# Three quarters of the second MLP's down-projection as 2x2 blocks in seven products

## The chip, the core and the metric

One core of one Trainium2 chip runs the whole program; the seven other cores are idle. The metric is the device time of one execution in microseconds (us). Five engines work side by side, each through its own list of instructions in a fixed order: TensorE (PE in the profile), VectorE (DVE), ScalarE (ACT), GpSimd (POOL) and SyncE (SP). SP issues the loads from DRAM, POOL issues other transfers besides small computations.

## The reference

A trunk of two layers on one sequence of 512 tokens of width 1024, in float32. Layer 0 mixes tokens by an mLSTM, layer 1 by a gated short convolution; each is followed by an MLP with squared ReLU. RMS norms stand before and behind each part.

```python
def sqrelu_mlp(x, w_up, w_down):
    h = jax.nn.relu(x @ w_up)
    return (h * h) @ w_down
...
        h = sqrelu_mlp(rms_norm(x, g[2]), w_mlp_up[i], w_mlp_down[i])
        x = x + rms_norm(h, g[3])
```

`w_up` is 1024 x 4096 and `w_down` 4096 x 1024. The change concerns `(h * h) @ w_down` of layer 1, where `h * h` is 512 x 4096.

## The kernel before

**Numbers.** Every large product is made from two reduced-precision halves: `split` (L79) writes the upper half of a tile on ScalarE (a cast, L80) and the remainder on VectorE (L81). `mm3` (L112) then makes three matmuls: upper times upper, upper times lower, lower times upper (L115, L116, L117). So each factor costs a ScalarE and a VectorE instruction, and each product three matmuls.

**Buffers.** `u` (15 tiles of 8 KB per partition) holds split weights, split activations and accumulators; `hb` (4 of 8 KB) the split hidden activations; `raw` (7 of 4 KB) weights as loaded; `t2` (8 of 2 KB) intermediate values. PSUM has eight banks of 512 columns: four named `pu`, two `pd`, two `pt`. A tile of a pool that is full waits until its oldest user is through.

**Up-projection.** The 4096 hidden columns are made by eight quads of 512 columns each (class `Quad`, L848). A quad is already a 2x2 block product in seven multiplications: the activations stand as seven factors (class `Seven`, L199: `a11`, `a12`, `a22`, `p1`, `n2`, `r3`, `p4`; seven `u` tiles that stay for the whole MLP), the weights as four blocks of 512 x 256 with four sums that VectorE forms from raw tiles (L957, L963, L981, L992). `prod` (L835) is one such product: 24 matmuls of 256 columns. Three quads begin early, during the layer before (`begin`, L885, the early product). For each finished quarter `take` (L1023) applies ReLU on ScalarE (L1026) where the values come from PSUM, squares on VectorE (L1029), and splits into an `hb` tile.

**Down-projection.** `down(g)` (L1040) multiplies the 512 hidden columns of quad g with 512 rows of `w_dn`: two column halves, four token tiles, four k tiles, three matmuls each, 96 matmuls of 512 columns (out `pd`). The weights come as four pieces of 128x1024, loaded (L98) and split. The result is written to accumulators `ys` by ScalarE for g = 0 (L1063) and added by VectorE after that (L1065). The order is quad 0, quad 1, `down(0)`, quad 2, `down(1)`, ..., `down(5)`, quad 7; `last_product` (L280) then takes the last 1024 hidden columns together with the norm and the store.

**Sums in DRAM.** During the first MLP, POOL's queue forms some sums of the convolution's weights in DRAM, for its quads (class `Sums`, L350): a tiny transfer (`mark`) that waits for an accumulator, so that the rest starts at the intended time, then copies from DRAM to DRAM and transfers that add. One such piece is made behind the first half of each of six `down(g)`.

**What sets the order.** The text above is traced in program order; a scheduler then fixes each engine's list when the program is built, from priorities and its own idea of durations. Each engine works its list strictly in order. A few items are put off by a count of TensorE time (`step`, `put_off`).

Of the kernel before, what the change touches and what calls it, by code (L numbers as in the profile page):

```python
# [39 lines left out]
def tile_hybrid_trunk(  # L40
# [309 lines left out]
    class Sums:  # L350

        def __init__(self, name, wm, c0, c1, shape, key, quads):
            self.all = dram.tile([2, 512] + shape, F32, name=name)

            def src(kh, c):
                m = wm[kh * 512 : (kh + 1) * 512, c : c + D]
                if len(shape) > 1:
                    m = m.rearrange("k (b s) -> k b s", s=512)[:, :, 0:256]  # L360
                return m

            self.blocks = src(0, c0), src(0, c1), src(1, c0), src(1, c1)
            for i, c in enumerate(quads):
                made[key, c] = [
                    self.of(n, i).rearrange("(p q) m -> q p m", q=P) for n in range(2)
                ]

        def of(self, n, i):
            f = self.all[n]  # L370
            return f[:, i, :] if len(f.shape) > 2 else f[:, i * 256 : (i + 1) * 256]

        def make(self, r0, r1, mark):

            a, b, c, d = (blk[r0:r1] for blk in self.blocks)
            f = [self.all[n, r0:r1] for n in range(2)]
            first = self.all[:, r0]
            first = first[:, 0, 0:1] if len(first.shape) > 2 else first[:, 0:1]
            nc.gpsimd.dma_start(first, mark)
            for dst, blk in zip(f, (a, b, d, c)):  # L380
                nc.gpsimd.dma_start(dst, blk)
            for dst, blk in list(zip(f, (b, d))) + []:
                nc.gpsimd.dma_start(dst, blk, accum_op=ALU.add, max_dma_last_dim=D)

    made = {}
# [404 lines left out]
        put_pair(hT, j, pr)  # L790

    wc = w_in_conv[0]
    cx = Sums("cx", wc, D, 2 * D, [D], "conv", [D + p * 256 for p in range(4)])
    og = Sums("og", wc, 0, 256, [2, 256], "conv", [0, 512])
    later = [(cx, p * P, (p + 1) * P) for p in range(4)] + [(og, 0, 256), (og, 256, 512)]

    def scores_and_core(t):
        scores(t)
# [218 lines left out]
    def mlp(i, xT, gain_of, tail_of, ends=False, ahead=None):  # L1017

        NG = FF // P // G
        hs = [None] * (FF // P // 2)  # L1020

        def quad(g):
            def take(nh, half, c, o):  # L1023
                j = 2 * g + nh
                if o is not None:
                    nc.scalar.activation(c, o, AF.Relu)  # L1026
                else:
                    o = c
                nc.vector.scalar_tensor_tensor(  # L1029
                    out=c, in0=o, scalar=0.0, in1=c, op0=ALU.max, op1=ALU.mult  # L1030
                )
# [8 lines left out]
        def down(g):  # L1040
            if g == 0:
                ys.extend(token_tiles())
            for hf, cs in enumerate(halves()):
# [6 lines left out]
                for t in range(NT):  # L1050
# [12 lines left out]
                        nc.scalar.copy(yh, o)  # L1063
                    else:
                        nc.vector.tensor_tensor(out=yh, in0=yh, in1=o, op=ALU.add)  # L1065
# [6 lines left out]
        gy, tail = gain_of(), tail_of()  # L1072
        quads[0].run_first()
        quads[1].run(True)
        for g in range(NG - 2):
            down(g)
            quads[g + 2].run(g + 2 < AHEAD)
            if g == NG - 4:
                fetch_x()
        last_product(w_dn[i], FF - D, hs[-(KO // 2) :], gy, tail, ys, ends, ahead)  # L1080


# [109 lines left out]
```

## Time and profile before

| | us |
|---|---|
| median of 3 runs | 1098.38 (1097.92 to 1098.44) |
| the profiled execution, its own time | 1098.65 |
| its span, first to last instruction | 1096.9 |
| TensorE busy | 1076.6 (98%) |
| VectorE busy | 744.8 (68%) |
| ScalarE busy | 503.9 (46%) |
| second MLP: early products from, quads 0 and 1 until, last product from | 748.9, 797.0, 1045.1 |

A group's row names the line, the engine, the operation, out<-in with shapes and count, then busy time and mean duration in ns, then the idle time of the engine ahead of these instructions and what ended it. A row of the order of time begins with start and duration, both in us, and ends with the wait in brackets. A row by window gives, for each engine, busy time and the instructions that touch the window, then granted TensorE clock, the busy share of the 16 DMA engines, and GB/s. Matmuls overlap, so the start-to-start distance counts, not their duration.

### The profile page before, as it was taken

Reading aid. Unit: us, or ns where it says so; the run is one execution under the profiler, and the core shown is the slowest. Engines: PE = TensorE matmul, PEld = TensorE weight load, DVE = VectorE, ACT = ScalarE, POOL = GpSimd, SP = SyncE. Lnnn points to the kernel's source line nnn. Section 1 sums busy time; section 2 is a strip of 40 time slices with the busy share of each in tenths; the row PEclk is TensorE's granted clock in tenths of the full one; section 3 lists DMA queues with packets and bytes.
Section 4 is the critical chain, followed back from the end, with each engine's and each line's share of the span. In section 5 each row is a group of like instructions: output and inputs, shape, how many; then the busy total and the mean of one; then the engine's idle time right before and its main releaser. Section 6 shows DMA issues by size and latency. Waiting matters only on the chain.

```text
span 1096.9 us, 16084 instructions
## 1 busy us (share of the span) xinstructions
PE 1076.6 (98%) x6531; PEld 948.9 (87%) x6531; DVE 744.8 (68%) x996; ACT 503.9 (46%) x780; POOL 98.1 (9%) x144
## 2 busy tenths in 40 slices
PE   8999999999999999999999999999999999999997
PEld 5878887789899898898888999988988988989986
DVE  5561567489775775766769978859967567565843
ACT  6431445355543353343556655646554424423521
POOL 1100010110001001011042000011000000000011
PEclk9999999999999999999999999999999999999999
DMA  8420273226386366385624554713533413415201
GB/s 269 135 77 1 63 244 126 86 97 192 116 230 178 110 173 156 109 256 134 211 76 138 188 194 137 249 58 124 175 125 97 154 51 104 136 56 193 96 20 58
DMA packets 114624, 147.90 MB, mean 135 GB/s; under 512 B 5845, under 2 KB 84469, under 8 KB 114550
## 3 DMA queue, kind: packets, MB, share of 16 engines
q1 hardware_dynamic: 101830, 118.03, 34.0%
q0 software_dynamic: 12720, 28.84, 9.4%
q8 instruction: 51, 0.84, 0.3%
q14 instruction: 23, 0.19, 0.1%
HBM read 138.47 MB, written 20.97 MB: 145 GB/s over the span
## 4 chain that ended last, share of the span: by engine, by line
PE 42%; DVE 4%; issue 2%; ACT 1%; DMA 1%; POOL 0%; POOLq 0%; DVEq 0%; ACTq 0%
PE pd L115 8%; PE pd L116 8%; PE pd L117 8%; PE pu L116 6%; PE pu L115 6%; PE pu L117 6%; DVE u L81 1%; DVE u L274 1%; PE pt L261 0%; ACT u L80 0%; DMA raw<-in_w_in_conv_dram 0%; POOL small L173 0%; DVE t L1029 0%; DMA xd<-u 0%; DVE hb L81 0%
## 5 line engine op out<-in xcount | busy, mean ns | idle before, releaser
L81 DVE TENSOR_TENSOR u<-raw,u 128x1024 fp32r<-128x1024 f32 (+1 forms) x270 | 320.7, 1200 | 126.5 <-ACT u L80 126.1
L80 ACT CAST u<-raw 128x1024 fp32r<-128x1024 f32 (+1 forms) x270 | 273.6, 1029 | 205.3 <-PE pd L117 159.8
L115 PE MATMUL pu<-u 128*128 128x256 f32 (+1 forms) x1112 | 336.8, 303 | 0.7 <-ACT u L80 0.7
L116 PE MATMUL pu<-u 128*128 128x256 f32 (+1 forms) x1112 | 335.5, 302 | 0.4 <-DVE u L81 0.4
L117 PE MATMUL pu<-u 128*128 128x256 f32 (+1 forms) x1112 | 334.4, 301 | 0.0
L115 PE MATMUL pd<-u,hb 128*128 128x512 f32 (+1 forms) x648 | 255.0, 393 | 1.5 <-DVE t L1029 0.9
L116 PE MATMUL pd<-u,hb 128*128 128x512 f32 (+1 forms) x648 | 254.1, 392 | 0.0
L117 PE MATMUL pd<-u,hb 128*128 128x512 f32 (+1 forms) x648 | 254.1, 392 | 0.0
L115 PEld LDWEIGHTS pu<-u 128*128 128x128 f32 x1112 | 210.2, 189 | 10.1 <-ACT u L80 1.1
L116 PEld LDWEIGHTS pu<-u 128*128 128x128 f32 x1112 | 209.9, 189 | 9.9 <-DVE u L81 1.3
L117 PEld LDWEIGHTS pu<-u 128*128 128x128 f32 x1112 | 210.0, 189 | 8.7 <-DVE u L81 0.3
L115 PEld LDWEIGHTS pd<-u,hb 128*128 128x128 f32 x648 | 121.8, 188 | 31.0 <-DVE t L1029 1.7
L117 PEld LDWEIGHTS pd<-u,hb 128*128 128x128 f32 x648 | 121.8, 188 | 28.0
L116 PEld LDWEIGHTS pd<-u,hb 128*128 128x128 f32 x648 | 121.8, 188 | 27.5 <-DVE u L81 0.6
L115 PE MATMUL pd<-u 128*128 128x256 f32 x312 | 88.3, 283 | 3.3 <-ACT pu L888 2.9
L116 PE MATMUL pd<-u 128*128 128x256 f32 x312 | 87.4, 280 | 0.0
L117 PE MATMUL pd<-u 128*128 128x256 f32 x312 | 87.2, 281 | 0.0
L1065 DVE TENSOR_TENSOR u<-u,pd 128x512 f32<-128x512 f32 x80 | 54.6, 683 | 36.6 <-PE pd L117 36.5
L181 ACT ACTIVATE junk<-u 128x512 bf16<-128x512 f32 (+1 forms) x49 | 30.5, 623 | 79.5 <-DVE u L318 58.1
L80 ACT CAST hb<-t 128x512 fp32r<-128x512 f32 x80 | 49.0, 620 | 32.5 <-DVE t L1029 26.6
L115 PEld LDWEIGHTS pd<-u 128*128 128x128 f32 x312 | 58.8, 188 | 4.4 <-ACT pu L888 3.6
L116 PEld LDWEIGHTS pd<-u 128*128 128x128 f32 x312 | 58.8, 189 | 0.0
(179 smaller groups left out, 864.9 us busy)
## 6 DMA issues: line engine op xcount, KB each, us to landing
raw<-in_w_mlp_up_dram SPq DMA_DIRECT2D x76, 512.0 KB, 5.0
raw<-in_w_mlp_down_dram SPq DMA_DIRECT2D x64, 512.0 KB, 4.0
raw<-in_w_in_mlstm_dram SPq DMA_DIRECT2D x24, 512.0 KB, 4.7
raw<-in_w_in_conv_dram SPq DMA_DIRECT2D x21, 512.0 KB, 4.9
cx<-in_w_in_conv_dram POOLq DMA_DIRECT2D x16, 512.0 KB, 6.5
xd<-u POOLq DMA_DIRECT2D x12, 512.0 KB, 3.1
u<-xd POOLq DMA_DIRECT2D x12, 512.0 KB, 6.9
raw<-in_w_out_mlstm_dram SPq DMA_DIRECT2D x8, 512.0 KB, 4.2
```

The lines of the kernel that those rows point to most:

```text
L80: hi = nc.scalar.copy(dst_hi, src)
L81: lo = nc.vector.tensor_tensor(out=dst_lo, in0=src, in1=dst_hi.bitcast(F32), op=ALU.subtract)
L115: nc.tensor.matmul(o, lh, rh, start=first, stop=False, skip_group_check=True)
L116: nc.tensor.matmul(o, lh, rl, start=False, stop=False, skip_group_check=True)
L117: nc.tensor.matmul(o, ll, rh, start=False, stop=last, skip_group_check=True)
L181: nc.scalar.activation(junk(n), src, AF.Square, scale=float(D) ** -0.5, accum_out=ms[:, i : i + 1])
L274: nc.vector.scalar_tensor_tensor(out=xt[:, hs], in0=y, scalar=r, in1=xt[:, hs], op0=ALU.mult, op1=ALU.add)
L1065: nc.vector.tensor_tensor(out=yh, in0=yh, in1=o, op=ALU.add)
```

## The change

For layer 1's MLP the first six `down(g)` become three calls of `down7(c)`, each for 1024 hidden columns (quads 2c and 2c+1) and 1024 rows of `w_dn`, ahead of quads 2, 4 and 6; quads 6 and 7 and `last_product` stay as they were. In `down7` the hidden activations are 2x2 blocks: `a11`, `a12`, `a21`, `a22`, with token halves as rows and quads as columns, and the weights 2x2 blocks of 512 x 512. Seven products of blocks replace eight: product 1 is a11 with the upper left weight block (banks x, two `pd`), 2 is a12 with the lower left one (added in x), 3 to 7 use differences of hidden blocks and sums of weight blocks (banks z, two `pt`; y, two `pu`; o, two `pd`). A product takes two loads and two splits of weights (two k tiles each), one split of a hidden block, and 2 token tiles x 4 k tiles x 3 = 24 matmuls of 512 columns. `minus` is a negated copy from banks to banks by ScalarE (L1151 of the new text), `add` adds banks to the accumulators (VectorE, L1143; for block 0, where a quarter is written for the first time, ScalarE, L1141), `plus` adds raw weights (VectorE, L1118), and L1160, L1164, L1173, L1178 are the differences of hidden blocks, formed in place.

For this the squares of quads 0 to 5 are written, unsplit, to two `u` tiles (`hb7`) by ScalarE (`take7`: ReLU, then Square), and VectorE's squaring and splitting there fall away. Two (blocks 1, 2) or four (block 0) sums of weight blocks are formed in DRAM on POOL's queue, behind the second half of the first MLP's six `down(g)`.

```diff
-            for dst, blk in list(zip(f, (b, d))) + []:
+            adds = list(zip(f, (b, d)))
+            if self.n > 2:
+                adds += [(f[2], f[0]), (f[3], f[2])]
+            for dst, blk in adds:
                 nc.gpsimd.dma_start(dst, blk, accum_op=ALU.add, max_dma_last_dim=D)
...
+    dn = [
+        Sums(f"dn{c}", n, [dn_block(c, kh, nh) for kh in range(2) for nh in range(2)], [512])
+        for c, n in enumerate((4, 2, 2))
+    ]
...
+        1: [(d, *r) for d in dn for r in halves_of],
...
+            def take7(nh, half, c, o):
+                h = hb7[g % 2][:, half, 2 * nh : 2 * nh + 2, :]
+                nc.scalar.activation(c, c if o is None else o, AF.Relu)
+                nc.scalar.activation(h, c, AF.Square)
+
+            if i == 1 and g < 6:
+                take = take7
...
-                if i == 0 and hf == 0 and later:
-                    sm, r0, r1 = later.pop(0)
-                    sm.make(r0, r1, yh[0:2, 0:1])
+                if i == 0 and later[hf]:
+                    sm, r0, r1 = later[hf].pop(0)
+                    sm.make(r0, r1, yh[0:4, 0:1])
+
+        def down7(c):
...
+            def mult(os, raws, fh, first):
+                for hh, raw in enumerate(raws):
+                    w = unit([2, 2, 512], F32R)
+                    split(w[:, 0], w[:, 1], raw)
+                    for u in range(2):
+                        step(PROD / 4)
+                        for k in range(2):
+                            mm3(
+                                os[u],
+                                [fh[:, s, 2 * hh + k, u * P : (u + 1) * P] for s in range(2)],
+                                [w[:, s, k, :] for s in range(2)],
+                                first and hh == 0 and k == 0,
+                                hh == 1 and k == 1,
+                            )
...
+            (a11, a12), (a21, a22) = a
+            x = two(pd)
+            mult(x, loads(dn_block(c, 0, 0)), factor_h(a11), True)
+            y = two(pu)
+            minus(y, x)
+            mult(x, loads(dn_block(c, 1, 0)), factor_h(a12), False)
+            add(0, 0, x)
+            tt(out=a21, in0=a21, in1=a22, op=ALU.subtract)
+            z = two(pt)
+            f5 = summed(0)
+            mult(z, f5, factor_h(a21), True)
+            tt(out=a11, in0=a11, in1=a21, op=ALU.subtract)
+            add(1, 1, z)
+            if sums.n > 2:
+                f6 = summed(2)
+            else:
+                d = loads(dn_block(c, 1, 1))
+                plus(f5, d)
+                f6 = f5
+            mult(y, f6, factor_h(a11), False)
+            tt(out=a12, in0=a12, in1=a11, op=ALU.subtract)
+            add(1, 0, y)
+            if sums.n > 2:
+                d = loads(dn_block(c, 1, 1))
+            mult(z, d, factor_h(a12), False)
+            tt(out=a11, in0=a22, in1=a11, op=ALU.subtract)
+            add(1, 0, z)
+            mult(y, summed(1), factor_h(a11), False)
+            o = two(pd)
+            minus(o, y)
+            add(1, 1, y)
+            if sums.n > 2:
+                f4 = summed(3)
+            else:
+                plus(f5, loads(dn_block(c, 1, 0)))
+                f4 = f5
+            mult(o, f4, factor_h(a22), False)
+            add(0, 1, o)
...
+            for k in range(2):
+                hb7[k] = unit([2, 4, 256])
+                nc.gpsimd.memset(hb7[k][:, 0, 0, 0:1], 0.0)
         quads[0].run_first()
         quads[1].run(True)
...
+            for g in range(2, NG):
+                if g % 2 == 0:
+                    down7(g // 2 - 1)
+                quads[g].run(g < AHEAD)
+            fetch_x()
```

**How the lists move.** Up to the second MLP, PE, DVE, ACT and SP keep the same rows in the same order; they keep them again in the last product. Three places follow; names ending in a number are buffers.

VectorE in the second `down(g)` and the quad after it, before: additions of `pd` banks to the accumulators (L1065) stand between the sums and splits of the next quad's weights.

```order
L81 TENSOR_TENSOR hb_7699<-t2_7730,hb_7699 128x512
L1065 TENSOR_TENSOR u_7429<-u_7429,pd_7745 128x512
L81 TENSOR_TENSOR u_7902<-raw_7867,u_7902 128x1024
L1065 TENSOR_TENSOR u_7429<-u_7429,pd_7759 128x512
L963 TENSOR_TENSOR raw_7867<-raw_7867,raw_7930 128x1024
L981 TENSOR_TENSOR raw_7869<-raw_7869,raw_7930 128x1024
L1065 TENSOR_TENSOR u_7430<-u_7430,pd_7773 128x512
L81 TENSOR_TENSOR u_7933<-raw_7867,u_7933 128x1024
```

VectorE now, at products 6 and 7 of block 1 (z is pt_8223 and pt_8224, y is pu_8179 and pu_8180; hb_8347 and hb_8392 are the hidden blocks of products 6 and 7, u_8395 and u_8410 the weights of product 7):

```order
L1143 TENSOR_TENSOR u_7461<-u_7461,pt_8223 128x512
L81 TENSOR_TENSOR hb_8347<-u_7138,hb_8347 128x1024
L1143 TENSOR_TENSOR u_7461<-u_7461,pt_8224 128x512
L1118 TENSOR_TENSOR raw_8225<-raw_8225,raw_8386 128x1024
L1118 TENSOR_TENSOR raw_8227<-raw_8227,raw_8388 128x1024
L81 TENSOR_TENSOR hb_8392<-u_7140,hb_8392 128x1024
L81 TENSOR_TENSOR u_8395<-raw_8225,u_8395 128x1024
L1143 TENSOR_TENSOR u_7462<-u_7462,pu_8179 128x512
```

The addition of a finished bank stands ahead of the split that the next product needs, and two sums of weights ahead of the next.

VectorE now, from there into quad 4 (o is pd_8380 and pd_8381; u_8431, u_8462 and u_8493 are the weights of quad 4's first three products):

```order
L81 TENSOR_TENSOR u_8410<-raw_8227,u_8410 128x1024
L1143 TENSOR_TENSOR u_7462<-u_7462,pu_8180 128x512
L81 TENSOR_TENSOR u_8431<-raw_8427,u_8431 128x1024
L970 TENSOR_TENSOR raw_8427<-raw_8427,raw_8429 128x1024
L1143 TENSOR_TENSOR u_7462<-u_7462,pd_8380 128x512
L1143 TENSOR_TENSOR u_7462<-u_7462,pd_8381 128x512
L81 TENSOR_TENSOR u_8462<-raw_8427,u_8462 128x1024
L994 TENSOR_TENSOR raw_8429<-raw_8429,raw_8490 128x1024
L976 TENSOR_TENSOR raw_8427<-raw_8427,raw_8490 128x1024
L81 TENSOR_TENSOR u_8493<-raw_8427,u_8493 128x1024
```

The additions of product 7's banks stand ahead of the splits for the quad's second and third products.

POOL in the first MLP, before, behind the first two `down(g)`: one piece of the convolution's sums `cx` each.

```order
L379 DMA cx<-u 2x1
L381 DMA cx<-in_w_in_conv_dram 128x1024 x2
L383 DMA cx<-in_w_in_conv_dram 128x4x256 x2
L379 DMA cx<-u 2x1
L381 DMA cx<-in_w_in_conv_dram 128x1024 x2
```

POOL now, at the same place (dn_711 is the tensor of block 0's sums):

```order
L364 DMA cx<-u 2x1
L366 DMA cx<-in_w_in_conv_dram 128x1024 x2
L371 DMA cx<-in_w_in_conv_dram 128x4x256 x2
L364 DMA dn_711<-u 4x1
L366 DMA dn_711<-in_w_mlp_down_dram 256x512 x4
L371 DMA dn_711<-in_w_mlp_down_dram 256x2x256 x2
L371 DMA dn_711<-dn_711 512x256 x2
L364 DMA cx<-u 2x1
```

Behind each of the convolution's pieces stands one of the sums for `w_dn`: eight transfers in the first two rounds, four in the four later ones.

More of the change, by code (lines that the diff above doesn't have):

```diff
@@ L350, in tile_hybrid_trunk, with __init__, make @@
     class Sums:
[L354 to L373, printed above, removed]
+        def __init__(self, name, n, blocks, shape):
+            self.n, self.blocks = n, blocks
+            self.all = dram.tile([n, 512] + shape, F32, name=name)
+        def make(self, r0, r1, marks):
             a, b, c, d = (blk[r0:r1] for blk in self.blocks)
[L376 removed]
+            f = [self.all[n, r0:r1] for n in range(self.n)]
             first = self.all[:, r0]
             first = first[:, 0, 0:1] if len(first.shape) > 2 else first[:, 0:1]
[L379 removed]
+            nc.gpsimd.dma_start(first, marks[0 : self.n, :])
             for dst, blk in zip(f, (a, b, d, c)):
                 nc.gpsimd.dma_start(dst, blk)
[L382 removed]
+            adds = list(zip(f, (b, d)))
+            if self.n > 2:
+                adds += [(f[2], f[0]), (f[3], f[2])]
+            for dst, blk in adds:
                 nc.gpsimd.dma_start(dst, blk, accum_op=ALU.add, max_dma_last_dim=D)
@@ L1065, in down, with factor_h, load_rows, loads @@
                         nc.vector.tensor_tensor(out=yh, in0=yh, in1=o, op=ALU.add)
-                if i == 0 and hf == 0 and later:
-                    sm, r0, r1 = later.pop(0)
-                    sm.make(r0, r1, yh[0:2, 0:1])
+                if i == 0 and later[hf]:
+                    sm, r0, r1 = later[hf].pop(0)
+                    sm.make(r0, r1, yh[0:4, 0:1])
+        def down7(c):
+            tt = nc.vector.tensor_tensor
+            a = [[hb7[k][:, half] for k in range(2)] for half in range(2)]
+            sums = dn[c]
+            def factor_h(src):
+                f = big.tile([P, 2, 4, 256], F32R, tag="hb", name="hb", bufs=NHB)
+                split(f[:, 0], f[:, 1], src)
+                return f
+            def load_rows(src, hh):
+                raw = raw_tile([2, 512])
+                nc.sync.dma_start(
+                    raw, src[hh * 256 : (hh + 1) * 256, :].rearrange("(k p) m -> p k m", p=P)
+                )
+                return raw
+            def loads(src):
+                return [load_rows(src, hh) for hh in range(2)]
+            def summed(n):
+                return loads(sums.all[n])
+            def plus(rs, qs):
+                for r, q in zip(rs, qs):
+                    tt(out=r, in0=r, in1=q, op=ALU.add)
+            def mult(os, raws, fh, first):
[11 more added lines that the diff above has]
+                                hh == 1 and k == 1,
+                            )
+            written = set()
+            def add(nh, half, os):
+                for u in range(2):
+                    yh = ys[2 * half + u][:, nh * 512 : (nh + 1) * 512]
+                    if c == 0 and (nh, half) not in written:
+                        nc.scalar.copy(yh, os[u])
+                    else:
+                        tt(out=yh, in0=yh, in1=os[u], op=ALU.add)
+                written.add((nh, half))
+            def two(bank):
+                return [bank() for _ in range(2)]
+            def minus(os, qs):
+                for o, q in zip(os, qs):
+                    nc.scalar.mul(o, q, -1.0)
+            (a11, a12), (a21, a22) = a
[31 more added lines that the diff above has]
+                f4 = summed(3)
+            else:
+                plus(f5, loads(dn_block(c, 1, 0)))
+                f4 = f5
+            mult(o, f4, factor_h(a22), False)
+            add(0, 1, o)
```

40 lines of the change are left out of this document (32 added, 8 removed).

## The prediction

> **What bounds the kernel now.** I read the page's first two parts, then the busy time by stage, then the groups of the second MLP by shape, then the order of time on each engine.
>
> ```profile
> span 1096.9 us, 16084 instructions
> PE 1076.6 (98%) x6531; PEld 948.9 (87%) x6531; DVE 744.8 (68%) x996; ACT 503.9 (46%) x780; POOL 98.1 (9%) x144
> PE   8999999999999999999999999999999999999997
> DVE  5561567489775775766769978859967567565843
> ```
>
> TensorE (PE) is busy from end to end; VectorE (DVE) is next at 68%, with its fullest slices where the second MLP starts. Busy is not peak, so I measured the pitch. The second MLP's second down-projection runs from 834.19 to 856.57 and the quad after it to 876.55:
>
> ```profile
> core 0: us, PE busy (x) PEld busy (x) DVE busy (x) ACT busy (x) POOL busy (x), PEclk, DMA share, GB/s
> 834.19:856.57 22.38, 22.38 (x98) 18.04 (x97) 15.70 (x20) 5.94 (x7) 0.00 (x0) 1.00 0.11 37
> 856.57:876.55 19.98, 19.98 (x170) 19.98 (x169) 13.86 (x16) 10.92 (x14) 0.00 (x0) 1.00 0.56 175
> 740.00:800.00 60.00, 58.60 (x446) 55.72 (x444) 56.31 (x75) 34.67 (x58) 4.26 (x6) 1.00 0.46 150
> ```
>
> A down-projection is 96 matmuls of 512 columns (two of the 98 only reach in), a quad 168 of 256: 22.38 / 96 = 0.2331 us and 19.98 / 168 = 0.119 us each, without a gap, at clock 1.00. So this stage is bound by the number of matmuls. VectorE needs 13.9 of a quad's 20 us there, but 56.3 of 60 us while the MLP starts, and even that costs TensorE 1.4 us only.
>
> **The matmuls removed.** Six down-projections are 576 matmuls. Three blocks of seven products, each 2 token tiles x 4 k tiles x 3, are 504, of the same 512 columns. 72 x 0.2331 = 16.8 us less TensorE time. By the Trainium skill (TensorE: Matmul & The Clock Gate, "Wait — 56ns, not 53.3ns?") matmuls start N / 2.4 GHz + 2.5 ns apart, 0.2158 us here; by it the saving would be 15.5 us, and the trace does not agree. I go by the trace.
>
> **What is added on VectorE and ScalarE (ACT).**
>
> ```profile
> L81 DVE TENSOR_TENSOR u<-raw,u 128x1024 fp32r<-128x1024 f32 x85 | 103.0, 1221 | 53.2 <-ACT u L80 53.1
> L1065 DVE TENSOR_TENSOR u<-u,pd 128x512 f32<-128x512 f32 x40 | 27.3, 683 | 18.4 <-PE pd L117 18.4
> L81 DVE TENSOR_TENSOR hb<-t,hb 128x512 fp32r<-128x512 f32 x32 | 21.8, 683 | 0.2 <-ACT hb L80 0.2
> L1029 DVE SCALAR_TENSOR_TENSOR t<-t 128x512 f32<-128x512 f32 x20 | 13.7, 685 | 0.2
> L963 DVE TENSOR_TENSOR raw<-raw 128x1024 f32<-128x1024 f32 x7 | 8.5, 1219 | 0.0
> L80 ACT CAST u<-raw 128x1024 fp32r<-128x1024 f32 x84 | 86.7, 1048 | 86.3 <-PE pd L117 76.4 <-DVE raw L957 7.3 <-DVE raw L992 1.1
> L1026 ACT ACTIVATE t<-pu 128x512 f32<-128x512 f32 x10 | 6.0, 598 | 14.5 <-PE pu L117 14.5
> L888 ACT ACTIVATE pu<-pu 128x512 f32<-128x512 f32 x6 | 3.5, 582 | 8.8 <-PE pu L117 8.8
> ```
> ```profile
> 807.84 3.50 DVE L81 TENSOR_TENSOR u<-raw,u 128x1024 fp32r<-128x1024 f32 x3 [5.98 <-ACT u L80]
> 736.92 1.29 DVE L81 TENSOR_TENSOR u<-pt,u 128x512 fp32r<-128x512 f32 x2 [1.00 <-ACT u L80]
> 758.02 0.58 ACT L888 ACTIVATE pu<-pd 128x512 f32<-128x512 f32 x1
> 758.54 2.93 ACT L80 CAST u<-raw 128x1024 fp32r<-128x1024 f32 x3
> 834.19 0.40 PE L115 MATMUL pd<-u,hb 128*128 128x512 f32 x1
> 834.42 0.40 PE L116 MATMUL pd<-u,hb 128*128 128x512 f32 x1
> ```
>
> Instructions in a row overlap a little: three splits take 3.50 us, not 3.67, so one more of 1024 elements costs (3.50 - 1.22) / 2 = 1.14 us and one of 512 costs 1.29 - 0.68 = 0.61; on ScalarE (2.93 - 1.05) / 2 = 0.95 for 1024, and for 512 the 0.52 from 758.02 to 758.54. A matmul lasts 0.40 us at a pitch of 0.23, so its result is there 0.17 us after the next could start.
>
> VectorE in blocks 1 and 2: 14 weight splits, 7 splits of hidden blocks, 4 differences of hidden blocks, 4 sums of weights, 29 x 1.14 = 33.1, and 12 additions into the accumulators, 12 x 0.61 = 7.3: 40.4 us beside 168 x 0.2331 = 39.2 us of TensorE. Block 0 has its weight sums from DRAM, and ScalarE writes eight of its twelve additions: 25 x 1.14 + 4 x 0.61 = 30.9 us. In exchange quads 0 to 5 lose four squarings and four splits each: 11 x 1.14 + 2 x 0.61 = 13.8 us instead of 18.6, in 20.0. A block with its two quads holds VectorE 58.5, 68.0 and (quads 6 and 7 keep their squarings) 77.6 us, against 79.2 us of TensorE; before, 8 x 1.14 + 16 x 0.61 + 2 x 18.6 = 56.1 against 84.7. ScalarE, with the squares (priced as L1026) and four negated copies (L888), has 21 x 0.95 + 4 x 0.52 = 22 us in a block (26 in block 0) and 7 x 0.95 + 12 x 0.52 = 13 in a quad, so it has room.
>
> The sum fits; the order decides. Of the 15 u buffers the seven activation factors take 7, the hidden blocks 2 and the accumulators 2; four are left, two products' worth, where six were left before. I walked VectorE's rows through block 1 with the durations above, each no earlier than the cast, the product or the freed buffer it needs, from TensorE's first product at 0:
> - First three products: the casts reach VectorE at 1.7, 3.95 and 7.35 us; the parts for products 3 and 4 are split by 8.5 and 15.8, needed from 11.2 and 16.8.
> - Product 5 (needed from 22.4): its hidden block is split at 20.4.
> - Product 6 (28.0): VectorE must first add bank z, complete at 26.8, and then split the hidden block: 28.6. TensorE's order puts the four matmuls that need only the upper half first, until 28.9: covered by 0.3.
> - Product 7 (33.6): two weight sums, the hidden split and the weight split end at 33.7; the first matmul needs only the cast: covered by 0.1.
> - The quad after it: the additions of product 7's banks end at 40.0; then come a split, two sums, a cast and a split, 45.5, where TensorE wants the lower half at 45.3 or so: 0.3 us lost.
>
> Blocks 0 to 2 thus lose 0, 0.3 and 0.3 us by the walk. For handovers that no row prices I take 0.7 us for each of blocks 1 and 2, 1.4 together. The bounds are a gain of 0.5 (VectorE's easier start of the MLP) and 5 us a block (first rival). The negated copy ahead of product 2 is ready at 4.9 and 6.4 us, the banks are wanted at 5.6 and 7.0: nothing, and 1.2 us per bank without this cover.
>
> ```profile
> 751.73 0.28 PE L117 MATMUL pd<-u 128*128 128x256 f32 x1
> 753.23 0.39 PE L115 MATMUL pd<-u 128*128 128x256 f32 x1 [1.22 <-ACT pu L888]
> 759.03 0.56 POOL L173 TENSOR_TENSOR small<-small,mhalf 128x1 f32<-128x1 f32 x1 [1.73 <-DVE small L168]
> ```
>
> POOL's two one-column memsets that claim the hidden blocks wait for the first early product, over at 752; the reciprocal root for the fourth token tile, which stands behind them, starts at 759: nothing.
>
> **What is added in the first MLP.** Only POOL's queue changes there: 32 transfers of 512 KB from DRAM to DRAM and six marks, behind the ones for the convolution.
>
> ```profile
> 296.00:338.00 42.00, 42.00 (x241) 36.60 (x241) 31.57 (x35) 18.97 (x25) 5.84 (x8) 1.00 0.66 185
> 338.00:380.00 42.00, 42.00 (x265) 37.68 (x264) 28.91 (x33) 16.85 (x21) 4.18 (x5) 1.00 0.54 148
> q0 software_dynamic: 8497, 13.62, 29.5%
> raw<-in_w_mlp_down_dram SPq DMA_DIRECT2D x23, 512.0 KB, 4.2
> raw<-in_w_mlp_up_dram SPq DMA_DIRECT2D x16, 512.0 KB, 8.6
> cx<-in_w_in_conv_dram POOLq DMA_DIRECT2D x12, 512.0 KB, 6.5
> og<-in_w_in_conv_dram POOLq DMA_DIRECT2D x8, 512.0 KB, 6.7
> u<-xd POOLq DMA_DIRECT2D x4, 512.0 KB, 7.3
> 333.39 0.56 POOL L379 DMA_DIRECT2D cx<-u  x1 [25.34 <-DVE u L1065]
> 341.44 2.65 POOL L383 DMA_DIRECT2D cx<-in_w_in_conv_dram  x2 [5.13 <-DMA cx<-in_w_in_conv_dram]
> 343.71 7.92 SPq L865 DMA_DIRECT2D raw<-in_w_mlp_up_dram  x4
> 354.14 23.72 SPq L98 DMA_DIRECT2D raw<-in_w_mlp_down_dram  x4
> 362.94 1.22 DVE L957 TENSOR_TENSOR raw<-raw 128x1024 f32<-128x1024 f32 x1
> ```
>
> The rows of queues and issues are of the 210 us from 310 to 520: q0 took 62 us of all engines for 12 + 8 + 4 transfers of 512 KB, 2.6 us each. The first two rounds of 42 us get eight more, 20.7 us, beside 0.66 x 42 = 27.7 and 22.7: 48 and 43 of 42, full. The four later rounds get 10.3 on about 23. So in two rounds weights land late. Their cover: loads issued from 343.71 on are first read at 362.94, 19 us later, for a landing of 8.6; those from 354.14 wait for buffers, not for engines. Twice the landing still fits: I take 0.5 us, bounds 0 and 4 a round. By the Trainium skill (DMA: Bandwidth & Descriptors, "Queues, rings and completion order") each engine goes round the queues packet by packet, so that q1 would keep half, and 8.6 would become at most about 17 us, an estimate from that rule; the up weights, which land in 8.6 us beside the convolution's sums where the down weights take 4.2, agree with it, and no run here shows a full round.
>
> **The sum.** Against the profiled run's own 1098.65 us (span 1096.9, 1.75 outside): 1098.65 - 16.8 + 1.4 + 0.5 = 1083.75. That run is 0.27 above the median of the three; forecast **1083.5 us**.
>
> **The rivals.**
> - VectorE sets the pace. If in blocks 1 and 2 nothing overlaps, 29 x 1.22 + 12 x 0.683 = 43.6 us, 4.4 more than TensorE; quads 6 and 7 then need 20.3, 0.3 more each. 1083.5 - 1.4 + 9.4 = 1091.5. For it: 77.6 of 79.2 us, and fewer buffers. Against it: 56.3 of 60 us cost 1.4 us.
> - Slower than before: the banks' handover. Four products of a block (2, 5, 6, 7) write banks that ScalarE or VectorE must read first. At 753.23 TensorE does wait for such a copy (L888), 1.22 us. The other bank's six matmuls cover 1.4 us. If the reader stands two splits behind, a handover costs 0.17 + 2 x 1.14 + 0.68 - 1.4 = 1.7 us, and some 0.3 at the second bank: 12 x 2.0 = 24, so 1083.5 - 1.4 + 24 = 1106. It decides from 16.8 / 12 = 1.4 us a handover on. Against it: the walk has readers at most 0.4 us late.
> - The sums in DRAM starve the first MLP: 8 us in its two full rounds, 1083.5 - 0.5 + 8 = 1091. Against it: the lead of 19 us.
>
> **How the numbers follow.** Forecast 0.68, VectorE 0.15, starved loads 0.07, handover 0.07; 0.03 for a mixture that just cancels the gain. Faster by over 0.2% (about what this kernel's runs can tell from no change): 0.68 + 0.15 + 0.07 = 0.90; within it 0.03; slower 0.07. The range starts at the full saving, 1098.38 - 16.8 - 0.5 = 1081, and takes in the first and third rival: 1081 to 1092; the forecast's own is 1081 to 1087.
>
> **What would show it.** Right: 72 matmuls fewer; each block near 39.3 us (block 0) and 39.5 to 40 (1 and 2); VectorE over 95% busy in blocks 1 and 2; TensorE's few waits there on L81 of hidden blocks and at the third product after a block; DMA share near 1 from 300 to 380 with TensorE still full. Wrong: blocks of 43 us or more with idle time before VectorE's splits (first rival), waits of over 1 us on L1151 or L1143 (second), or TensorE idle between 300 and 380 (third).

## The result, and the profile after

| | before | after |
|---|---|---|
| median of the runs, us | 1098.41 (1097.92 to 1098.65, 4 runs) | 1086.72 (1083.68 to 1087.24, 4 runs) |
| profiled execution, us (its span) | 1098.65 (1096.9) | 1083.68 (1082.0) |
| matmuls | 6531 | 6459 |

The ratio is 0.9888, with a 95% interval of 0.987 to 0.9907: 11.7 us faster, and 1086.72 us against 1083.5 forecast. The profiled run gained 15.0 us, the three others (1086.61, 1086.83, 1087.24) about 12. The same kernel in a later series had a median of 1088.26 (1087.47 to 1089.06; ratio 0.991, 0.9897 to 0.9924). So 3 to 5 us come and go, and the questions are where, and why.

The page of the change, its head and the DMA row of the slices:

```profile
span 1082.0 us, 16129 instructions
PE 1060.0 (98%) x6459; PEld 934.8 (86%) x6459; DVE 775.5 (72%) x995; ACT 555.8 (51%) x847; POOL 133.6 (12%) x186
...
DMA  9420274225399998798953556632555424524601
```

TensorE is full as before, on 72 matmuls fewer. The slices from the twelfth to the twentieth (297 to 541 us), where the first MLP runs, show DMA at 0.7 or more. Then the second MLP by stage, first of before (from the first down-projection to the last product), then of the change (block 0, its two quads, block 1, and so on):

```profile
797.04:1045.13 248.09, 247.71 (x1539) 221.22 (x1537) 169.66 (x192) 107.90 (x137) 2.15 (x4) 1.00 0.34 110
```
```profile
797.45:836.63 39.18, 39.18 (x171) 31.53 (x170) 34.48 (x32) 27.20 (x34) 0.00 (x0) 1.00 0.53 164
836.63:870.78 34.15, 34.15 (x289) 34.15 (x288) 23.42 (x22) 24.35 (x34) 0.00 (x0) 1.00 0.47 153
870.78:910.04 39.26, 39.26 (x170) 31.45 (x169) 37.68 (x38) 21.62 (x25) 0.00 (x0) 1.00 0.42 135
910.04:950.48 40.44, 40.00 (x337) 39.77 (x336) 31.41 (x29) 28.66 (x40) 0.00 (x0) 1.00 0.41 130
950.48:989.75 39.27, 39.27 (x170) 31.46 (x169) 37.68 (x38) 21.69 (x25) 0.00 (x0) 1.00 0.42 135
989.75:1030.00 40.25, 39.85 (x338) 39.64 (x336) 37.56 (x41) 27.79 (x37) 2.15 (x4) 1.00 0.49 171
```

The blocks take 39.18, 39.26 and 39.27 us without a gap; the stage takes 232.55 us (797.45 to 1030.00) in place of 248.09, 15.5 us less. VectorE is busy for 37.68 of 39.27 us in blocks 1 and 2, 96%. The waits of TensorE from 500 to 1040 us in the change (engine, line, what it waited for; us in total, times, the longest):

```profile
PE pd L115 <- DVE u L318: 2.0, 1, 2.0
PE pd L115 <- ACT pu L901: 1.6, 2, 1.2
PE pt L261 <- DVE t L252: 1.4, 1, 1.4
PE pu L115 <- ACT u L80: 0.8, 2, 0.4
```

The second and third were there before. The fourth are the third products of the quads after blocks 1 and 2. The first is new and stands in the first MLP, at its last product (L318 adds the finished product to the accumulator and so frees the bank). These are instructions of the change on ScalarE there, and TensorE's wait:

```profile
528.11 1.05 ACT L80 CAST u<-raw 128x1024 fp32r<-128x1024 f32 x1 [2.22 <-DMA raw<-in_w_mlp_down_dram]
530.91 1.05 ACT L80 CAST u<-raw 128x1024 fp32r<-128x1024 f32 x1 [1.76 <-DMA raw<-in_w_mlp_down_dram]
532.74 1.05 ACT L80 CAST u<-raw 128x1024 fp32r<-128x1024 f32 x1 [0.78 <-DMA raw<-in_w_in_conv_dram]
533.69 0.61 ACT L80 CAST hb<-t 128x512 fp32r<-128x512 f32 x1
...
542.63 0.50 PE L115 MATMUL pd<-u,hb 128*128 128x512 f32 x1 [2.01 <-DVE u L318]
```

ScalarE waits four times for weights that have not landed, 5.2 us in all; the three longest are shown. Behind them, in its fixed order, stands the cast of a hidden block (533.69; before it was at 530.10), so VectorE's split of that block is some 3 us later than before, and 5 us later counted from TensorE, which at 510 us was 1.4 us ahead of before. The addition L318 is late too, and TensorE finds its bank taken. What the loads met is in POOL's queue, first of before, then of the change:

```profile
503.47 1.78 POOL L381 DMA_DIRECT2D og<-in_w_in_conv_dram  x2 [1.31 <-DMA og<-u]
```
```profile
510.28 1.77 POOL L366 DMA_DIRECT2D og<-in_w_in_conv_dram  x2 [9.55 <-DMA og<-u]
515.20 1.35 POOL L371 DMA_DIRECT2D og<-in_w_in_conv_dram  x1 [3.16 <-DMA og<-in_w_in_conv_dram]
...
532.00 1.15 POOL L366 DMA_DIRECT2D dn<-in_w_mlp_down_dram  x2 [13.35 <-DMA dn<-u]
```

The convolution's last piece (`og`) waits 9.55 us for its mark in place of 1.31, behind the fifth piece of sums and a fetch of four token tiles (`u<-xd`) which that piece delays. So its adding transfers run from 515.20 on, beside the weights, whose loads are issued from 513.48 on. The last piece of sums makes its first copies at 532.00, after ScalarE's waits for the last product's weights (524.83 to 530.91): in this profile it is not what held those up.

And the DMA share (last column but one) of the first MLP's two full rounds in the change, then of its end in before and in the change:

```profile
296.00:338.00 42.00, 42.00 (x241) 36.65 (x240) 30.19 (x33) 18.87 (x24) 10.66 (x12) 1.00 0.98 259
338.00:380.00 42.00, 42.00 (x266) 37.63 (x265) 28.90 (x33) 16.85 (x21) 12.13 (x14) 1.00 0.94 234
```
```profile
506.00:530.00 24.00, 24.00 (x185) 23.04 (x184) 19.63 (x22) 16.84 (x20) 2.73 (x2) 1.00 0.92 251
530.00:548.00 18.00, 18.00 (x83) 14.65 (x82) 10.33 (x13) 5.68 (x11) 2.57 (x2) 1.00 0.50 153
```
```profile
506.00:530.00 24.00, 24.00 (x188) 23.19 (x187) 19.09 (x20) 15.13 (x18) 4.99 (x5) 1.00 0.84 227
530.00:548.00 18.00, 15.99 (x69) 12.53 (x68) 9.24 (x12) 7.51 (x12) 6.86 (x6) 1.00 0.99 276
```

The two rounds that I had worked out to be full are full, and TensorE stands still for not a moment. The round at the end was 0.92 full for 24 us already before the change; the added transfers pushed work past 530, into the loads for the last product and for the convolution.

### The profile page after: what moved, and what is told of

Same layout as the page of the kernel before. It is cut to its first block, busy times and chain, and to the rows that moved or that the text cites. A ratio compares the mean times of both kernels' runs of the same rounds, so it can differ in the third digit from the quotient of the medians.

```text
span 1082.0 us, 16129 instructions
## 1 busy us (share of the span) xinstructions
PE 1060.0 (98%) x6459; PEld 934.8 (86%) x6459; DVE 775.5 (72%) x995; ACT 555.8 (51%) x847; POOL 133.6 (12%) x186
## 5 line engine op out<-in xcount | busy, mean ns | idle before, releaser
L81 DVE TENSOR_TENSOR u<-raw,u 128x1024 fp32r<-128x1024 f32 (+1 forms) x288 | 342.1, 1201 | 102.9 <-ACT u L80 102.3
L80 ACT CAST u<-raw 128x1024 fp32r<-128x1024 f32 (+1 forms) x288 | 292.7, 1030 | 171.9 <-PE pd L117 85.4
L115 PE MATMUL pd<-u,hb 128*128 128x512 f32 (+1 forms) x528 | 207.7, 393 | 3.1 <-DVE u L318 2.0
L116 PE MATMUL pd<-u,hb 128*128 128x512 f32 (+1 forms) x528 | 206.9, 392 | 0.0
L117 PE MATMUL pd<-u,hb 128*128 128x512 f32 (+1 forms) x528 | 206.7, 392 | 0.0
L115 PEld LDWEIGHTS pd<-u,hb 128*128 128x128 f32 x528 | 99.2, 188 | 27.2 <-DVE u L318 2.5
L117 PEld LDWEIGHTS pd<-u,hb 128*128 128x128 f32 x528 | 99.2, 188 | 22.9 <-DVE hb L81 0.2
L116 PEld LDWEIGHTS pd<-u,hb 128*128 128x128 f32 x528 | 99.3, 188 | 22.6 <-DVE u L81 0.8
L115 PEld LDWEIGHTS pd<-u 128*128 128x128 f32 x312 | 58.7, 188 | 4.3 <-ACT pu L901 3.4
L116 PEld LDWEIGHTS pd<-u 128*128 128x128 f32 x312 | 58.8, 189 | 0.0
L117 PEld LDWEIGHTS pd<-u 128*128 128x128 f32 x312 | 58.6, 188 | 0.0
L80 ACT CAST hb<-t 128x512 fp32r<-128x512 f32 x56 | 34.3, 619 | 23.0 <-DVE t L1043 17.3
```

Of the source, the lines that this page charges most:

```text
L80: hi = nc.scalar.copy(dst_hi, src)
L81: lo = nc.vector.tensor_tensor(out=dst_lo, in0=src, in1=dst_hi.bitcast(F32), op=ALU.subtract)
L115: nc.tensor.matmul(o, lh, rh, start=first, stop=False, skip_group_check=True)
L116: nc.tensor.matmul(o, lh, rl, start=False, stop=False, skip_group_check=True)
L117: nc.tensor.matmul(o, ll, rh, start=False, stop=last, skip_group_check=True)
```

## The experiments

My theory after the result: the second MLP runs as forecast, and what varies is lost at the end of the first MLP, where the sums in DRAM hold up loads of weights. The rival: the blocks of the second MLP lose it, in the runs that have no profile.

### The change again, and without its sums in DRAM

`again` is the change unaltered. `no_sums`:

```diff
-        1: [(d, *r) for d in dn for r in halves_of],
+        1: [],
...
-                return loads(sums.all[n])
+                return loads(dn_block(c, *((0, 1), (1, 0), (1, 1), (0, 0))[n]))
```

> The change once more, for the spread of its times. Theory (the loads of weights at the end of the first MLP are held up by the sums in DRAM): the profiled run of 1083.68 us lost 2.0 us at the first MLP's last product, the timed runs of 1086.6 to 1087.2 lost about 5 there, so times between 1083 and 1088, and in a run near 1087 a wait of TensorE of 4 to 5 us around 540 us. Rival (the second MLP's blocks lose the other 3 us): in a run near 1087 the blocks are 1 us longer each and the wait around 540 stays at 2.

> The change without a sum of the second MLP's weights in DRAM: the blocks load plain blocks of w_mlp_down in their place (the output is not the reference's), everything else as in the change. Theory: no wait at the end of the first MLP, and the blocks unchanged: 1098.4 - 16.8 + 1.2 (the waits of 0.60 and 0.55 us after blocks 1 and 2) - 0.5 (the easier start) = 1082.0, between 1081 and 1082.7, with a spread of under 1 us. Rival: the blocks set the loss, so 1084.5 or more and as wide a spread as the change has.

Measured: `again` 1088.26 us, profiled in a run of 1089.06; `no_sums` 1083.03 (1082.54 to 1083.33; ratio 0.9862, 0.9849 to 0.9876). The blocks of `again` are those of the first run: its waits after blocks 1 and 2 are 0.45 and 0.40 us. Its end of the first MLP is not:

```profile
535.06 1.05 ACT L80 CAST u<-raw 128x1024 fp32r<-128x1024 f32 x1 [3.35 <-DMA raw<-in_w_in_conv_dram]
...
540.19 0.50 PE L115 MATMUL pd<-u,hb 128*128 128x512 f32 x1 [0.62 <-ACT hb L80]
546.39 0.50 PE L115 MATMUL pd<-u,hb 128*128 128x512 f32 x1 [2.88 <-DVE u L318]
547.43 0.43 PE L116 MATMUL pd<-u,hb 128*128 128x512 f32 x1
547.66 0.62 PE L117 MATMUL pd<-u,hb 128*128 128x512 f32 x1
...
551.07 0.39 PE L116 MATMUL pd<-u,hb 128*128 128x512 f32 x1
...
548.00:550.00 2.00, 2.00 (x6) 1.53 (x5) 0.00 (x0) 0.00 (x0) 2.00 (x2) 0.50 1.14 188
```

The wait is 2.88 us in place of 2.01, there is one of 0.62 ahead of it, and then a third loss that is no wait at all: from 547.66 to 550.64 the matmuls last 0.6 us in place of 0.4, at a granted clock of 0.50. From 547.43 to 551.07 nine matmuls start in 3.64 us where nine pitches are 2.10: 1.5 us. Together with the two gaps (0.78 and 3.04 beyond the pitch) that is 5.4 of the 6.5 us by which this run is behind the profiled run of `no_sums`. Another 0.6 us was there in the first 18 us. The theory holds, the rival falls. `no_sums` came out 0.3 us above the range that I gave (the terms named there give 1082.3, not 1082.0), but without the loss and narrow.

Not all that comes and goes is lost there, though. Of the 5.4 us between the two profiles of the change, 3.5 lie at the end of the first MLP and 1.7 in the program's first 18 us: the second group of eight transposes (L261) starts at 16.31 in the first profile, at 18.04 in `again`, at 17.79 in before, and at 17.25 to 18.17 in the eleven other profiles. Why the first profile was ahead there is open, and where the runs without a profile lose their time is inferred from these two.

### The sums alone, on the kernel before

`before_sums` has the change's transfers and marks in the first MLP of the kernel before, with nothing to read them:

```diff
...
+        1: [(d, *r) for d in dn for r in halves_of],
...
+                if i == 0 and later[hf]:
+                    sm, r0, r1 = later[hf].pop(0)
+                    sm.make(r0, r1, yh[0 : 4 if hf else 2, 0:1])
```

> The kernel before, with the change's 32 transfers and six marks for the sums of the second down-projection's weights in the first MLP, where nothing reads them. Theory: slower than before by what the first MLP loses, 2 to 5 us: 1100.5 to 1103.5, with a wait of TensorE at the first MLP's last product. Rival: within 1 us of before, 1098 to 1099.5.

Measured: 1104.27 us (1101.36 to 1104.94) beside 1098.31 of before, ratio 1.0048 (1.0035 to 1.0062): 6.0 us for the sums alone, above my bound of 5. Its profile shows the waits of `again` almost to the hundredth (0.63 and 2.87 us), and a granted clock of 0.50 behind them.

### One block's sums made elsewhere

`dn2_in_conv` issues the third block's two pieces in the convolution, with the convolution's fresh accumulators as marks:

```diff
-        1: [(d, *r) for d in dn for r in halves_of],
+        1: [(d, *r) for d in dn[:2] for r in halves_of],
+        2: [(dn[2], *r) for r in halves_of],
...
+                if p in (0, 1):
+                    sm, r0, r1 = later[2].pop(0)
+                    sm.make(r0, r1, ys[0][0:4, 2 * p + 1, 0:1])
```

> The change with the sums for the third block (two pieces, eight transfers of 512 KB, two marks) issued in the convolution's first two quads in place of the first MLP's last two rounds. Theory: the last rounds of the first MLP have the kernel before's transfers again, TensorE's wait around 540 us goes, and the time is that without sums to within 0.5 us: 1081.5 to 1082.7. Rival (it is the whole row of sums, which puts POOL's queue behind for 200 us): 1083 to 1085. If the second MLP loses the 3 us: 1084.5 or more.

Measured: 1082.62 us (1082.46 to 1082.91), ratio 0.9859 (0.9846 to 0.9873): the whole loss is gone, and the scatter with it. Four of six pieces still go through the first MLP, at a share of 0.89 from 296 to 506 us, and cost nothing. So it is not the sums as such, nor POOL's long queue, but their place.

### Only one of the two pieces moved

`last_piece` moves the very last piece alone, `fifth_piece` the one before it alone.

```diff
-        1: [(d, *r) for d in dn for r in halves_of],
+        1: [(d, *r) for d in dn for r in halves_of][:5],
+        2: [(dn[2], *halves_of[1])],
...
```
```diff
-        1: [(d, *r) for d in dn for r in halves_of],
+        1: [(d, *r) for d in dn[:2] for r in halves_of] + [None, (dn[2], *halves_of[1])],
+        2: [(dn[2], *halves_of[0])],
...
```

> The change with only the very last piece of sums (third block, lower half) moved from the first MLP's last round to the convolution's first quad. Theory (POOL's queue is behind by then, so that the convolution's last piece runs late and meets the weight loads of the last quad, whatever comes after it): a wait stays around 540 us, shorter than before: 1083 to 1087. Rival (the last piece's own transfers, which run until 545 us, do it): no wait, 1082.3 to 1082.9, as with both pieces moved.

> The counterpart: only the last but one piece of sums (third block, upper half, issued from 483 us on) moved to the convolution's first quad, the very last one left in the first MLP. Theory (the last but one piece holds POOL's queue up, so that the fetch of the four token tiles and the convolution's last piece run 10 us late and into the weight loads that start around 513): both are on time again, the wait around 540 goes or is under 1 us: 1082.3 to 1084. Rival (any piece too many in the last two rounds does it): 1085 to 1089 as with the last one moved.

Measured: `last_piece` 1088.26 us (1087.15 to 1089.86), `fifth_piece` 1088.01 (1086.08 to 1090.29). For `last_piece` my expectation held: a wait of 2.88 us stays. For `fifth_piece` it did not: the convolution's last piece was on time again, as I had said, and yet its profile has a wait of 4.92 us. With the way free, the last piece went through earlier and met the loads all the same:

```profile
519.41 1.14 POOL L366 DMA_DIRECT2D dn<-in_w_mlp_down_dram  x2 [5.87 <-DMA dn<-u]
...
530.08 1.05 ACT L80 CAST u<-raw 128x1024 fp32r<-128x1024 f32 x1 [3.11 <-DMA raw<-in_w_mlp_down_dram]
...
540.74 1.05 ACT L80 CAST u<-raw 128x1024 fp32r<-128x1024 f32 x1 [2.81 <-DMA raw<-in_w_in_conv_dram]
```

So the rival as I had put it stands: either piece is one too many for the last two rounds, the fifth because it delays the convolution's last piece into the loads, the last because it runs into them itself once the way is free.

### The order of ScalarE in place of the transfers

`conv_casts_last` leaves all six pieces in place and moves three casts on ScalarE, with VectorE's halves of those splits: the ones for the convolution's first weights, which had stood between the last hidden blocks' casts.

```diff
...
-            qd.prepare()
+            if qd.key == "conv":
+                raw = qd.block(0, 0)
+                with tc.issue_after(made["hid"]):
+                    qd.f1 = qd.factor(raw)
+            else:
+                qd.prepare()
...
-                split(hs[j][:, 0, half], hs[j][:, 1, half], c)
+                made["hid"] = split(hs[j][:, 0, half], hs[j][:, 1, half], c)[0]
```

> The change with all six pieces of sums left in the first MLP, and one edit in the order of ScalarE and VectorE there: the splits of the convolution's first three weight blocks stand behind the split of the first MLP's last hidden block, not between the last hidden blocks (nothing else moves on ScalarE). Theory (the transfers are late, but what stops TensorE is that ScalarE, which works in order, waits for weights which the convolution reads later, and the hidden blocks' casts stand behind them; in the second run of the change 4.8 of its 7.1 us of such waits were for the convolution's weights and 2.3 for the last product's own): most of the loss goes, 1082.6 to 1084.8. Rival (the last product's own weights are late enough): 1086 to 1089, as the change.

Measured: 1083.85 us (three runs of 1083.50 to 1084.12, one of 1086.88), ratio 0.9877 (0.9861 to 0.9894). In the profiled run (1084.12) ScalarE still waits 2.56 us for the convolution's weights, but now with nothing behind it that TensorE needs soon:

```profile
533.36 1.22 ACT L80 CAST hb<-t 128x512 fp32r<-128x512 f32 x2 [0.86 <-DVE t L1048]
...
538.38 1.05 ACT L80 CAST u<-raw 128x1024 fp32r<-128x1024 f32 x1 [2.56 <-DMA raw<-in_w_in_conv_dram]
...
542.83 0.51 PE L115 MATMUL pd<-u,hb 128*128 128x512 f32 x1 [0.40 <-DVE u L318]
...
506.00:545.00 39.00, 38.60 (x249) 34.67 (x248) 30.11 (x33) 22.94 (x30) 6.27 (x8) 1.00 0.99 288
```

The transfers are busier than in any other run of the table below (0.99), and TensorE waits 0.40 us. Another 0.8 us goes at 567 us, which the table's last column does not reach: transposes (L261) wait for ScalarE (0.51 and 0.20 us), and whether the moved casts cause that is open. Side by side, with ScalarE's waits for landings from 505 to 545 us (505 to 550 in the last row) and what the matmuls between 520 and 560 us take longer than the same ones of before, slow clock included, each of one profiled run:

| | DMA share, 506 to 545 | ScalarE waits for landings | TensorE loses | median |
|---|---|---|---|---|
| before | 0.79 | 0 | 0 | 1098.4 |
| no_sums | 0.79 | 1.2 | 0 | 1083.0 |
| dn2_in_conv | 0.78 | 0.2 | 0 | 1082.6 |
| the change, first profile | 0.88 | 5.2 | 2.3 | 1086.7 |
| the change, `again` | 0.95 | 7.1 | 5.8 | 1088.3 |
| last_piece | 0.89 | 6.4 | 6.3 | 1088.3 |
| fifth_piece | 0.90 | 8.0 | 7.2 | 1088.0 |
| conv_casts_last | 0.99 | 5.2 | 0.7 | 1083.9 |

Late landings are the cause, and what turns them into lost time is a queue in fixed order, in which a prefetch for the next layer stands ahead of this layer's operand. How much of the waiting is for that prefetch differs: 4.8 of 7.1 us in `again`, 0.8 of 5.2 in the first profile of the change, where 4.4 were for the last product's own weights, which the order of the casts does not help. The run of 1086.88 also suggests that this order is not all of it; it has no profile, and the loads for the last product itself (2.0 us of waits in the profiled run) may be what is left.

### VectorE in the second MLP

Four runs priced the other side. `late_add`, `dve_squares` and `two_sums` stand on `dn2_in_conv`, `dve_sums` and `dve_both` on the change without its sums in DRAM.

`late_add`, in blocks 1 and 2 (`made["last"]` is the next quad's sum for its third product, L977):

```diff
...
-            add(0, 1, o)
+            def last_add():
+                with tc.issue_after(made["last"].ins):
+                    add(0, 1, o)
+            if c == 0:
+                add(0, 1, o)
+            else:
+                put_off(2 * PROD + 0.1, last_add)
```

> The kernel with the third block's sums in the convolution, and in blocks 1 and 2 the two additions of the seventh product put behind the sum of weights for the next quad's third product (one edit in VectorE's order). Theory (the third product waits because these two additions, 0.68 us each, and a wait of 0.4 for the banks stand ahead of that sum): the waits of 0.60 us after blocks 1 and 2 go, 1082.6 - 1.2 = 1081.4, between 1081.0 and 1081.9. Rival (the whole row of VectorE is late there, so another instruction is late next): 1082.3 to 1083.

Measured: 1081.66 us (1081.49 to 1081.88), ratio 0.9846 (0.9832 to 0.9861), 1.0 us less than `dn2_in_conv`: the best version of this work, faster than both kernels. VectorE's row after block 1, first of `dn2_in_conv`, then of `late_add` (L1144 are the two additions, L977 the sum that the third product needs):

```profile
908.11 0.68 DVE L1144 TENSOR_TENSOR u<-u,pd 128x512 f32<-128x512 f32 x1
909.19 0.69 DVE L1144 TENSOR_TENSOR u<-u,pd 128x512 f32<-128x512 f32 x1 [0.40 <-PE pd L117]
...
912.07 1.22 DVE L977 TENSOR_TENSOR raw<-raw 128x1024 f32<-128x1024 f32 x1
```
```profile
911.24 1.22 DVE L977 TENSOR_TENSOR raw<-raw 128x1024 f32<-128x1024 f32 x1
912.38 1.28 DVE L1144 TENSOR_TENSOR u<-u,pd 128x512 f32<-128x512 f32 x2
```

TensorE's waits after the blocks are gone from its list, and nothing else came up.

`dve_squares` and `two_sums`:

```diff
-                nc.scalar.activation(c, c if o is None else o, AF.Relu)
-                nc.scalar.activation(h, c, AF.Square)
+                if o is not None:
+                    nc.scalar.activation(c, o, AF.Relu)
+                else:
+                    o = c
+                nc.vector.scalar_tensor_tensor(
+                    out=h, in0=o, scalar=0.0, in1=c, op0=ALU.max, op1=ALU.mult
+                )
```
```diff
-        for c, n in enumerate((4, 2, 2))
+        for c, n in enumerate((2, 2, 2))
```

> The kernel with the third block's sums in the convolution, and the squares of quads 0 to 5 on VectorE again (24 instructions of 512 elements, some 0.61 us each, 14.6 us more VectorE and 14.6 less ScalarE). Theory (VectorE has room in the quads, 16.2 of 20 us, and is tight only where a block hands over to a quad): the waits after blocks grow by at most a squaring or two each, 1082.6 to 1085. Rival (VectorE sets the pace of this MLP as soon as it has more to do): 1087 to 1095.

> The kernel with the third block's sums in the convolution, and block 0 with two sums from DRAM like blocks 1 and 2 (eight transfers of 512 KB fewer in the first MLP's first two rounds, four sums of 1.14 us more on VectorE in block 0, no longer 30.9 but 35.5 us of 39.2). Theory: block 0 still fits, and the two full rounds cost nothing as it is, so no change: 1082.3 to 1083.3. Rival (four sums are too much for block 0): 1084 to 1087.

Measured: 1082.68 us (1081.93 to 1083.42) and 1082.99 (1082.66 to 1083.56), beside 1082.62 of their base: no difference. The quads have room for the squares, and block 0 for four more sums. Two parts of the change, squares on ScalarE and four sums for block 0, were not needed, each taken alone; both left out together was not run.

`dve_sums` makes all sums on VectorE, `dve_both` the squares as well:

```diff
...
-        1: [(d, *r) for d in dn for r in halves_of],
+        1: [],
...
-                return loads(sums.all[n])
+                f = loads(dn_block(c, *((0, 0), (1, 1))[n]))
+                plus(f, loads(dn_block(c, 0, 1)))
+                return f
```

> The change without sums in DRAM, all four sums of weights of a block made by VectorE from plain blocks (two loads and two additions more for each, so four additions of 1.14 us more in blocks 1 and 2, eight in block 0). VectorE then has 29 x 1.14 + 4 x 1.14 + 7.3 = 44.9 us in blocks 1 and 2, and 40 in block 0, beside 39.2 us of TensorE, and 72.5 with two quads, beside 79.2. Theory (four free buffers hold two products' work, so a block can't borrow much from the quads): blocks 1 and 2 lose 2 to 6 us each, 1086 to 1093 in all. Rival (the first MLP alone was hurt, VectorE has room): 1082.3 to 1084, and then the sums in DRAM were not needed.

> As the last, with the squares of quads 0 to 5 on VectorE too: 44.9 us in blocks 1 and 2, 16.2 in a quad, 77.4 with two quads beside 79.2. Theory: what the blocks push back meets fuller quads, 1 to 4 us more than with the squares on ScalarE. Rival (the squares never mattered, as with the sums in DRAM): the same to within 0.5 us.

Measured: `dve_sums` 1094.55 us (1093.94 to 1098.58), ratio 0.9969 (0.9958 to 0.9981); `dve_both` 1098.53 (1096.21 to 1101.28), ratio 0.9999 (0.999 to 1.0008). Blocks 1 and 2 of `dve_sums`, TensorE's waits from 797 to 1005 (L1153 is the negated copy), and VectorE's first sum of weights for block 1 (L1120):

```profile
872.20:918.47 46.27, 41.52 (x170) 32.31 (x169) 44.21 (x45) 25.46 (x30) 0.00 (x0) 0.96 0.54 170
958.79:1003.00 44.21, 41.57 (x171) 32.31 (x170) 42.09 (x42) 23.57 (x28) 0.00 (x0) 0.96 0.53 171
...
PE pu L116 <- DVE u L81: 4.0, 2, 2.0
PE pd L115 <- ACT pu L1153: 3.3, 4, 2.4
...
870.54 1.23 DVE L1120 TENSOR_TENSOR raw<-raw 128x1024 f32<-128x1024 f32 x1 [3.92 <-DMA raw<-in_w_mlp_down_dram]
```

Four sums more in a block and it takes 46.3 and 44.2 us with VectorE busy for 95% of it, though it has room over a block and its two quads together. VectorE is not the whole of it: the sums need four loads more, and for the first of them VectorE waits 3.92 us ahead of block 1 and 1.81 ahead of block 2, and about 1.5 us in each block is the slow clock behind a wait of 2.02 us. The run does not part the loads from the additions. The blocks lose 7.0 and 4.9 us, one above and one within the 2 to 6 that I expected; the total is 1.5 us above my range. The squares cost 4.0 us more on such blocks, at the end of the range given. Against this way of making them, the sums in DRAM buy 11.9 us (1094.55 - 1082.62), or 11.2 with each run set against before in its own series.

## Why the prediction was right, point by point

- **The matmuls removed, 16.8 us, and the handovers, 1.4.** Together 15.4; from the first two quads to the last product the profiled run took 15.8 us less (15.5 in the stage shown, 0.3 in the two quads ahead of it). The blocks were within 0.2 us of 39.3, and the waits came where the walk had put them, at the third product of the quad after a block. They are the part that was mis-sized inside: the walk said 0.3 us each, the runs 0.55 to 0.60 with the pitch taken off, and nothing anywhere else, in place of 0.7 each with an allowance for handovers. TensorE waits there for a cast (L80) that hangs on VectorE's sum, not for the lower half as in the walk, and the waits on hidden blocks (L81) that I had named did not come; `late_add` shows that the additions ahead of that sum are the cause.
- **VectorE.** Forecast 40.4 us of work in blocks 1 and 2, measured 37.68 in the block and the rest in the quad; for block 1 and its quads 68.0 forecast, 69.1 measured; block 0 58.5 and 57.9. The first rival's price, VectorE without overlap, did not come about. `dve_sums` shows how near its condition was: four additions, with their loads, more in a block.
- **The second rival,** the banks' handover: no wait on L1151 or L1143 in any block of the change. In `dve_sums`, where ScalarE's negated copy comes late, it did appear (3.3 us on L1153).
- **What is added in the first MLP, 0.5 us.** This is the step that was wrong. The two rounds that I called full are full (0.98 and 0.94) and cost nothing, by the lead of 19 us that I named; there the bound of 0 held. But the sentence "The four later rounds get 10.3 on about 23" fits only two of them: before the change the four have DMA shares of 0.55, 0.54, 0.67 and 0.74 of 42 us. The last is some 31 us, 41 of 42 with 10.3 more, and it holds a stretch at 0.92 before anything is added. The term measured 2.3 us in the profiled run, 5.8 in the second; `before_sums` was 6.0 us slower. The third rival had the right mechanism (landings late), the wrong place (300 to 380 in place of 510 to 545) and 8 us. That the profiled run agreed with the sum to 0.1 us was luck: 1.8 us too little for the first MLP stood against 0.4 us more gain in the second than forecast, and 1.5 us less in the first 18 us of the program, which the change does not touch.
- **The rule weighed there.** By the Trainium skill (DMA: Bandwidth & Descriptors, "Queues, rings and completion order") each engine goes round the queues packet by packet, from which I had estimated landings of up to 17 us. In the two full rounds the medians, first of before, then of the change, stay far below:

```profile
cx<-u POOLq DMA_DIRECT2D x3, 0.0 KB, 1.6
raw<-in_w_mlp_up_dram SPq DMA_DIRECT2D x8, 512.0 KB, 9.7
```
```profile
raw<-in_w_mlp_down_dram SPq DMA_DIRECT2D x9, 512.0 KB, 8.6
raw<-in_w_mlp_up_dram SPq DMA_DIRECT2D x8, 512.0 KB, 5.9
dn<-u POOLq DMA_DIRECT2D x2, 0.0 KB, 11.8
```

  At the end of the first MLP, where they cost time, single loads of weights took up to 14.6 us (`again`).

## What to carry to other kernels

A transfer that is "free" is free in a stretch: read the DMA share in windows of a round over the whole region that the added transfers can reach, the last round above all, and not as a mean. Where a prefetch for the next stage shares an engine in fixed order with this stage's operands, a late landing stops this stage; putting the prefetch's first use behind the operands (three casts here) took 4.4 us off, and moving two of six pieces into a slacker stage 5.6, each against the change's second median. And before two engines' work is shifted to make room, try whether there is room: the squares, or four of the sums, could have stayed.

## What the runs showed of the hardware that I had not expected

- **A gap of two to three microseconds can cost more than its length.** After TensorE's wait of 2.88 us in `again` the granted clock fell to 0.50 for 3.4 us, 1.5 us more lost; in `dve_sums` two waits of 2.02 us were followed by the same, the first of them in the row below. After the wait of 2.01 us in the first profile and one of 2.37 us in `dve_sums` (at 880.35) the clock stayed at 1.00:

```profile
907.00:909.00 2.00, 2.00 (x7) 1.52 (x6) 2.00 (x3) 0.54 (x1) 0.00 (x0) 0.50 0.78 233
```

  The Trainium skill (TensorE: Matmul & The Clock Gate, "Part 1: The HAM clock gate (the "warmup" mystery)") says that the clock falls to half after at least one idle window of about 3.4 us, and that the window runs freely. In these traces the length of the gap alone does not decide, and gaps well under 3.4 us were enough.
- **A transfer of four elements lands behind the one ahead of it in its queue.** Before, the marks of the two full rounds landed in 1.6 us (median), with nothing of POOL's queue ahead of them. In the change the marks of the new sums took 7.6 to 14.3 us, and each landed 0.2 us after the transfer ahead of it in POOL's queue: the last, issued at 517.44, at 531.72, behind an adding transfer of the convolution's that landed at 531.50. Each of POOL's pieces begins by waiting for its mark, so a late piece delays the next and pushes it into a later stage.
- **The loss scatters between runs.** With the same instructions the end of the first MLP cost 2.3 us in one profile and 5.8 in another, and the kernels with this loss spread over 1.6 to 4.2 us, against 0.4 to 1.5 for `dn2_in_conv` and the three that stand on it, and 0.7 to 1.9 for before. One profile of such a kernel says little about its median.
